# Cross-attention queries computed by rows, partly in seven products, and turned by transposes; third head's keys ahead of the first values

## The chip, the cores and the metric

The kernel runs on one core of a Trainium2 chip. The metric is the device time of one execution in microseconds (us), as a median of several runs. A profile is one further execution, recorded by the hardware profiler; its span goes from the first to the last instruction. The engines are named as the profile does: PE (TensorE, matrix products; PEld its weight loads), DVE (VectorE), ACT (ScalarE), POOL (GpSimd) and SP (SyncE, which issues the DMAs).

## What is computed

One encoder block on x (256 rows of 2048) with memory mem (256 rows of 2048), all in f32:

```python
x = x + 0.5 * swiglu(rms_norm(x, ffn1_norm), w_gate, w_up, w_down)      # 2048 -> 5632 -> 2048
x = x + concat(pool_mixer, gla_mixer)(rms_norm(x, mix_norm) @ w_in) @ w_out
x = x + mem_cross_attention(rms_norm(x, xattn_norm), rms_norm(mem, mem_norm), w_q, w_kv, w_o)
x = x + 0.5 * swiglu(rms_norm(x, ffn2_norm), ...)
out = rms_norm(x, final_norm)

def mem_cross_attention(h, mem_h, w_q, w_kv, w_o):      # 4 heads of 512
    q = (h @ w_q).reshape(b, s, 4, 512)
    kv = (mem_h @ w_kv).reshape(b, 256, 2, 4, 512)
    k, v = kv[:, :, 0], kv[:, :, 1]
    p = softmax(einsum('bshd,bmhd->bhsm', q, k) * 512 ** -0.5)
    return einsum('bhsm,bmhd->bshd', p, v).reshape(b, s, 2048) @ w_o
```

The change touches the cross-attention alone.

## The kernel before

**Products in f32.** Each f32 operand is split into a rounded part and a remainder (`split`, L705: ACT casts to fp32r, DVE subtracts). A product is then three products in fp32r: high by high, high by low and low by high. The activations lie split in `xs` and `ys`, as 16 tiles of 128 features with 256 tokens, high and low side by side. Weights come from DRAM as units of 1 MB into four buffers `raw`; DVE and ACT split a unit into `wh` and `wl`.

**Three ways to go through a weight.** `block_a` (L746) works by columns: a unit is 4 tiles of features by 512 columns, the weights stand in the array, the tokens stream, and the result `pa` has features on partitions. Each of a unit's 16 weight tiles needs one product of 512 columns (high and low tokens) and one of 256 (the weights' remainder). `block_s` (L889) works by rows: a unit is 2 tiles of features by 1024 columns, 128 tokens at a time stand in the array, the weights stream, and the result `pt` has tokens on partitions. A plain unit is 24 products of 512 columns. For the pairs of tiles that its argument `pairs` names, a unit goes by sevens: a scheme like Strassen's, 7 block products instead of 8, so 21 products of 512. This needs sums of the activations (`part_sums`, L818, on DVE, in tiles `xe`, `ye` or `xx`) and sums of the weights (`split_seven`, L842: `xh` and `xl` hold the split of three quarters of the raw unit, three DVE additions make the sums in `raw`, and these are split into `wh` and `wl`). When the last such unit is done, `combine` (L967) copies and adds the extra accumulators into a tile of its own, and each half of the result is later joined with the plain accumulators on DVE (`joined_to`, L1186). The accumulators come from four PSUM tiles of two banks; a block by rows with sevens holds all four until `combine` has read two of them.

**Cross-attention before.** Four heads of queries by columns (L1726 to L1730): `ev_Q` (L1660) adds the two halves of each accumulator into a tile `c` (ACT copy, DVE add) and splits that into `ys`. Then mem, normalized by rows, is transposed into `xs` a quarter at a time (`mem_fold`, L1619, tiles `tm`), each quarter as soon as the last query block has read the tiles that it overwrites. Keys by columns into `K` (`ev_K`), logits, softmax and its transposes per head (`logits`, `probs`), values by rows with pairs 2, 4 and 6 by sevens (`V_PAIRS`, L1201), and `values` (`pv`) per head. The sequence is keys 0, keys 1, values of heads 0 and 1, keys 2, keys 3, values of heads 2 and 3.

**What sets the order.** The program is a stream of units with operations hung between them: `st.op(f, n)` runs f after n further units. From it `Plan` (L205) makes a list of tasks and orders every engine's instructions by a model of their costs and due times; TensorE takes, of the tasks that the model holds ready, the first in program order. So the whole program is ordered anew when a part of it changes. Tiles of a stage live in a scope of memory that is opened and closed with it; the cross-attention's is `s_x` (L1646: one `xh` and `xl`, three tiles `c`). Nearly all instructions carry line L552, the recorder's, so rows are told apart by their tiles.

Of the kernel before, what the change touches and what calls it, by code (L numbers as in the profile page):

```python
# [10 lines left out]
F32 = mybir.dt.float32  # L11
# [6 lines left out]
P = 128  # L18
# [548 lines left out]
def build(ctx, tc, I, out):  # L567
# [24 lines left out]
    def local(shape, dt, tag, name, bufs=1):  # L592
        return tile_of(None, shape, dt, tag, name, bufs)
# [33 lines left out]
    def ctl(name, shape):  # L627
        return whole_lines(const, shape, F32, name, name)
# [4 lines left out]
    ident = plan.fixed(eye, [P, P])  # L633
    gains = ctl("gains", [P, G_END])
    Rcol = ctl("Rcol", [P, 2])
    ss = ctl("ss", [P, 2, 8])
    sums = ctl("sums", [P, 2])
    chain = ctl("chain", [P, 3, 8])

# [247 lines left out]
                )  # L887

    def block_s(srcs, act, ext, pairs, evict, spare=None, joins=(0, 1), delays=(0, 0), order=None,  # L889
                ends=None):  # L890

# [73 lines left out]
            ends.row_factor(1)  # L965

        def combine():  # L967
            e = held["e"] = local([P, 4, NB], F32, tag="sg", name=uid("sg"), bufs=2)
            a, b = held["parts"]
            nc.scalar.copy(e[:, 0], a[:, 0])  # L970
            nc.vector.tensor_tensor(out=e[:, 3], in0=a[:, 1], in1=e[:, 0], op=ALU.add)
            nc.vector.tensor_tensor(
                out=e[:, 1:3], in0=b, in1=e[:, 3:4].to_broadcast([P, 2, NB]), op=ALU.add
            )
            nc.vector.tensor_tensor(out=e[:, 3], in0=b[:, 1], in1=e[:, 1], op=ALU.add)
            held["rest"] = {j: (e[:, 2:4], ALU.subtract) if j else (e[:, 0:2], ALU.add) for j in joins}
# [221 lines left out]
    END_ORDER = (0, 2, 1, 4, 3, 5)  # L1198
    OUT_PAIRS = (3, 4, 6)
    W_OUT_PAIRS = (3, 5, 6)  # L1200
    V_PAIRS = (2, 4, 6)  # L1201

    def sums_of(act, ext, pairs, tag, forms=3):
        t = local([P, len(pairs), 2, forms, P], F32R, tag=tag, name=uid(tag))
# [7 lines left out]
    def gate_sums():  # L1212

        sums_of(xs, xe, PAIRS, "xe")

    def ffn(wg, wu, wd, down, first=()):
        gate = {}

        def hidden():
            e = local([P, 4, NB], F32, tag="sg", name=uid("sg"), bufs=2)  # L1220
            return {0: e[:, 2:4], 1: e[:, 0:2]}

        def ev_gate(j, c, fresh):
# [12 lines left out]

        def turn(g, k):

            v = four(ptile(uid("ph")))
            for i in range(4):  # L1240
                for h in range(2):
                    nc.tensor.transpose(
                        v[:, i, h * P : (h + 1) * P], g[:, h, i * P : (i + 1) * P], ident
                    )
            split(ys[:, k : k + 4, 0, :], ys[:, k : k + 4, 1, :], v)

        for lo, n in FF_PARTS:
            for b in range(0, n - 1, 2):
                n0 = (lo + b) * NB
                pairs = first if lo == b == 0 else PAIRS  # L1250
                if pairs:
                    block_s(wwide(wg, n0), xs, xe, pairs, joined_to(lambda j, c: ev_gate(j, c, 0)))
                else:
                    block_t(wwide(wg, n0), xs, lambda j, ps: ev_gate(j, ps, 1))
                block_s(wwide(wu, n0), xs, xe, PAIRS, joined_to(ev_up))
                held = {}
                st.op(lambda held=held: held.update(gate))
                wait = PAIRS[-1] + 1 if b + 2 < n else 1
                for j in range(2):
                    st.op(lambda j=j, b=b, held=held: turn(held[j], 4 * (b + j)), wait)  # L1260
                if not b and (lo + n < FF // NB or down is down_first):
                    st.op(lambda: sums_of(ys, ye, DOWN_PAIRS, "ye"), wait)
            if n % 2:
                def both(j, c):
                    if j:
                        ev_up(0, c)
                    else:
                        ev_gate(0, c, 0)
                block_s(wtwo(wg, wu, (lo + n - 1) * NB), xs, xe, PAIRS, joined_to(both), joins=(0, 1))
                st.op(lambda n=n: turn(gate[0], 4 * (n - 1)), 1)  # L1270
            down(wd, 4 * lo, 4 * n, lo + n == FF // NB)
# [323 lines left out]
    st.op(open_scope("s_out"), 1)  # L1595


    xa = {}

    def xt(name, shape, dt=F32, tag=None, bufs=1):  # L1600
        t = whole_lines(None, shape, dt, tag or name, uid(name), bufs)
# [8 lines left out]
    def mem_norm():  # L1610
        for c in range(8):
            row_squares([xa[f"mem{h}"][:, c * S : (c + 1) * S] for h in range(2)], c)
        nc.vector.tensor_reduce(out=sums, in_=ss, axis=AX.X, op=ALU.add)
        Rm = xt("Rm", [P, 2])
        rsqrt(Rm, sums, D, 2)
        for h in range(2):
            nc.vector.tensor_scalar_mul(xa[f"mem{h}"], xa[f"mem{h}"], Rm[:, h : h + 1])
# [12 lines left out]

    xx = {}

    def mem_sums(g):
        if not xx:
            xx["all"] = local([P, len(V_PAIRS), 2, 4, P], F32R, tag="xx", name=uid("xx"))
        i = V_PAIRS.index(g)
        xx[g] = xx["all"][:, i]
        part_sums(xs, xx["all"][:, i : i + 1], (g,))

    def x_factors():  # L1640
        nc.vector.tensor_scalar_mul(xt("nR", [P, 2]), Rcol, -(XHD ** -0.5))
        nc.vector.tensor_scalar_mul(xt("sR", [P, 2]), Rcol, XHD ** -0.5)

    into_x(I["w_out"][0], ys, 1.0, G_X, spread_too=False, pairs=W_OUT_PAIRS, made=1)
    st.op(close_scope, 2)
    st.op(open_scope("s_x", 1, 3), 2)  # L1646
    st.op(x_factors, 2)
    st.op(mem_in, 2)
    st.op(mem_norm, 6)
# [4 lines left out]
    def whole(ps):  # L1654
# [1 line left out]
        nc.scalar.copy(c, ps[:, :, S:])  # L1656
        nc.vector.tensor_tensor(out=c, in0=ps[:, :, :S], in1=c, op=ALU.add)
        return c

    def ev_Q(h):  # L1660
        def evict(p, ps):
            split_pair(ys, 4 * h + 2 * p, whole(ps))
        return evict

    def ev_K(h):
        def evict(p, ps):
# [13 lines left out]
    def logits(h):  # L1680
        ps = ptile(uid("pl"))
        for t in range(2):
            tok = slice(t * P, (t + 1) * P)
            parts = [(d, a, b) for d in range(4) for a, b in ((0, 0), (0, 1), (1, 0))]
            for i, (d, a, b) in enumerate(parts):
                nc.tensor.matmul(
                    ps[:, t, :M], ys[:, 4 * h + d, a, tok], xa["K", h][:, d, b, :],
                    start=i == 0, stop=i == 11,
                )
        nm, sm = xt("nm", [P, 2]), xt("sm", [P, 2])  # L1690
        nc.vector.tensor_reduce(out=nm, in_=ps[:, :, :M], axis=AX.X, op=ALU.max)
        nc.vector.tensor_tensor(out=nm, in0=nm, in1=xa["nR"], op=ALU.mult)
        pr = xt("P", [P, 2, M])
        for t in range(2):
            nc.scalar.activation(
                pr[:, t, :], ps[:, t, :M], AF.Exp, scale=xa["sR"][:, t : t + 1],
                bias=nm[:, t : t + 1], accum_out=sm[:, t : t + 1],
            )
        nc.vector.reciprocal(out=sm, in_=sm)
        for t in range(2):  # L1700
            nc.vector.tensor_scalar_mul(pr[:, t, :], pr[:, t, :], sm[:, t : t + 1])

    def probs(h):
        ps = ptile(uid("pt"))
        for mtile in range(2):
            for t in range(2):
                nc.tensor.transpose(
                    ps[:, mtile, t * P : (t + 1) * P], xa["P"][:, t, mtile * P : (mtile + 1) * P], ident
                )
        PT = xa["PT", h] = xt("PT", [P, 2, 2, S], F32R, bufs=2)  # L1710
        split(PT[:, :, 0, :], PT[:, :, 1, :], ps[:, :, :S])

    def values(h):
# [9 lines left out]
                    )  # L1723
            split_pair(ys, 4 * h + 2 * p, ps[:, :, :S])

    for h in range(H):  # L1726
        if h == H - 1:
            for c in range(4):
                st.op(lambda c=c: mem_fold(c), c + 2)
        block_a(wblock(w_q, h * NB), xs, ev_Q(h))  # L1730
    for b in range(2):
        h = 2 * b
        block_a(wblock(w_kv, h * NB), xs, ev_K(h))
        if not b:
            for i, g in enumerate(V_PAIRS):
                st.op(lambda g=g: mem_sums(g), 1 + i)
        st.op(lambda h=h: logits(h), 2)
        st.op(lambda h=h: probs(h), 3)
        block_a(wblock(w_kv, (h + 1) * NB), xs, ev_K(h + 1))
        st.op(lambda h=h: logits(h + 1), 1)  # L1740
        st.op(lambda h=h: probs(h + 1), 2)
        block_s(wwide(w_kv, D + h * NB), xs, xx, V_PAIRS, joined_to(ev_V(b)))
        for j in (0, 1):
            st.op(lambda h=h, j=j: values(h + j), 1)
# [169 lines left out]
```

## Time and profile before

| | |
|---|---|
| median of 3 runs | 2077.27 us (2076.41 to 2078.64) |
| the profiled execution, its own time | 2078.63 us |
| its span | 2076.5 us, granted TensorE clock 0.999 |
| busy: PE, PEld, DVE, ACT | 2064.3, 1730.3, 1822.4, 1151.6 us |
| cross-attention up to the last `pv` | about 993 to 1291 us of the span |
| DMA | 436 MB, 210 GB/s |

How to read it: a row of a group gives engine, operation, output<-inputs, shape, count, busy us, mean ns of one, and the idle time before with what ended it. A matmul's mean is its time from entry to modelled end; as they are pipelined, their pace is the distance between starts. A row of waits reads waiter <- what it waited for: us, times, longest. A row of the chain or of the timeline begins with its start and its length in us.

### The profile page before, as it was taken

The numbers are of one execution on the slowest core, as the hardware profiler recorded it, in microseconds if no ns is written. First come the engines' busy times: TensorE is split into PE (matmuls) and PEld (weight loads), VectorE is DVE, ScalarE is ACT, GpSimd is POOL, SyncE is SP. The second block draws the span as 40 slices with busy tenths as digits, with TensorE's granted clock in tenths as the row PEclk, the third lists the DMA queues.
The fourth block names the chain that finished last, engine by engine and source line by source line (L and its number), as shares of the span: only waits on it lengthen the run. The fifth ranks groups of instructions, "written<-read, shape, count | busy, mean of one in ns | idle before, by whom it ended". The sixth has DMA issues, their size and how long they took to land.

```text
span 2076.5 us, 24457 instructions
## 1 busy us (share of the span) xinstructions
PE 2064.3 (99%) x9846; PEld 1730.3 (83%) x9846; DVE 1822.4 (88%) x1618; ACT 1151.6 (55%) x1058; POOL 7.2 (0%) x37
## 2 busy tenths in 40 slices
PE   9999999999999999999999999999999999999998
PEld 7888888888888888888888888888888888888887
DVE  7999899998999977689767758998998999989996
ACT  7665455654555655456655445656554556554654
POOL 0000000000000000000000000000000000000000
PEclk9999999999999999999999999999999999999999
DMA  8556765566656755556754545665467655676564
GB/s 303 185 202 219 247 213 210 174 253 223 229 183 237 248 187 183 166 174 234 274 181 165 201 145 179 223 241 205 164 222 263 223 186 192 232 245 221 188 237 142
DMA packets 139640, 436.07 MB, mean 210 GB/s; under 512 B 9924, under 2 KB 13608, under 8 KB 139144
## 3 DMA queue, kind: packets, MB, share of 16 engines
q1 hardware_dynamic: 139208, 433.99, 60.7%
q8 instruction: 77, 1.26, 0.2%
q10 hardware_dynamic: 320, 0.53, 0.1%
q14 instruction: 35, 0.29, 0.0%
HBM read 417.71 MB, written 16.78 MB: 209 GB/s over the span
## 4 chain that ended last, share of the span: by engine, by line
PE 81%; DVE 13%; DMA 2%; ACT 2%; issue 2%; SPq 0%; DVEq 0%; ACTq 0%
PE pt L552 61%; PE pa L552 15%; DVE wl L552 5%; DVE raw L552 3%; PE pb L552 2%; DVE xl L552 2%; DVE sg L552 1%; DMA raw<-in_ffn_w_down 1%; ACT wh L552 1%; PE ph L552 1%; DMA raw<-in_ffn_w_up 1%; PE px L552 1%; PE pl L552 1%; PE pv L552 1%; ACT xh L552 0%
## 5 line engine op out<-in xcount | busy, mean ns | idle before, releaser
L552 ACT CAST wh<-raw 128x2048 fp32r<-128x2048 f32 (+2 forms) x383 | 719.3, 1886 | 570.9 <-DVE raw L552 330.2
L552 DVE TENSOR_TENSOR wl<-raw,wh 128x2048 fp32r<-128x2048 f32 (+2 forms) x382 | 856.3, 2259 | 127.3 <-ACT wh L552 124.9
L552 PE MATMUL pt<-wh,xs 128*128 128x512 f32 x2028 | 656.0, 390 | 0.0
L552 PE MATMUL pt<-wh,ys 128*128 128x512 f32 x1508 | 477.4, 389 | 0.8 <-DVE ys L552 0.5
L552 PEld LDWEIGHTS pt<-wh,xs 128*128 128x128 f32 x2028 | 379.9, 188 | 78.7 <-DVE xs L552 0.7
L552 PE MATMUL pt<-wl,xs 128*128 128x512 f32 x1014 | 395.4, 390 | 0.4 <-DVE wl L552 0.2
L552 PEld LDWEIGHTS pt<-wh,ys 128*128 128x128 f32 x1508 | 282.7, 188 | 59.8 <-DVE ys L552 0.9
L552 DVE TENSOR_TENSOR raw<-raw 128x1024 f32<-128x1024 f32 x360 | 312.2, 867 | 8.6
L552 PE MATMUL pt<-wl,ys 128*128 128x512 f32 x754 | 293.0, 389 | 0.1
L552 ACT CAST xh<-raw 128x1536 fp32r<-128x1536 f32 x120 | 176.8, 1481 | 99.3 <-PE pt L552 38.9
L552 DVE TENSOR_TENSOR xl<-raw,xh 128x1536 fp32r<-128x1536 f32 x120 | 210.2, 1752 | 18.0 <-ACT xh L552 17.8
L552 PEld LDWEIGHTS pt<-wl,xs 128*128 128x128 f32 x1014 | 190.4, 188 | 42.6 <-DVE wl L552 3.2
L552 PE MATMUL pa<-xs,wh 128*128 128x512 f32 x912 | 220.4, 392 | 0.0
L552 PEld LDWEIGHTS pa<-xs,wh 128*128 128x128 f32 x912 | 167.2, 188 | 32.6 <-issue 0.3
L552 PEld LDWEIGHTS pt<-wl,ys 128*128 128x128 f32 x754 | 141.6, 188 | 29.6 <-DVE wl L552 0.8
L552 DVE TENSOR_TENSOR sg<-pt,sg 128x1024 f32<-128x1024 f32 (+1 forms) x155 | 149.6, 966 | 14.4 <-ACT sg L552 12.6
L552 PE MATMUL pt<-wh,xe 128*128 128x512 f32 x380 | 139.6, 390 | 0.0
L552 PE MATMUL pt<-xh,xs 128*128 128x512 f32 x344 | 120.1, 390 | 0.0
L552 PEld LDWEIGHTS pa<-xs,wl 128*128 128x128 f32 x896 | 115.0, 191 | 4.4
L552 PE MATMUL pa<-xs,wl 128*128 128x256 f32 x896 | 116.4, 283 | 0.0
L552 PEld LDWEIGHTS pt<-wh,xe 128*128 128x128 f32 x380 | 71.3, 188 | 15.0
L552 PEld LDWEIGHTS pt<-xh,xs 128*128 128x128 f32 x344 | 64.6, 188 | 13.4
(210 smaller groups left out, 1575.9 us busy)
## 6 DMA issues: line engine op xcount, KB each, us to landing
raw<-in_ffn_w_down SPq DMA_DIRECT2D x88, 1024.0 KB, 5.4
raw<-in_ffn_w_up SPq DMA_DIRECT2D x80, 1024.0 KB, 5.1
raw<-in_ffn_w_gate SPq DMA_DIRECT2D x77, 1024.0 KB, 5.0
raw<-in_w_in SPq DMA_DIRECT2D x32, 1024.0 KB, 5.3
raw<-in_xattn_w_kv SPq DMA_DIRECT2D x32, 1024.0 KB, 5.2
raw<-in_w_out SPq DMA_DIRECT2D x16, 1024.0 KB, 5.4
raw<-in_xattn_w_q SPq DMA_DIRECT2D x16, 1024.0 KB, 6.8
raw<-in_xattn_w_o SPq DMA_DIRECT2D x16, 1024.0 KB, 5.4
```

The costliest lines, as they stand in the source:

```text
L552: return f(*(real(a) for a in args), **{k: real(a) for k, a in kw.items()})
```

## The change

Queries go by rows: two blocks of 1024 columns, the first with pairs 4 and 6 by sevens, the second with 2, 4 and 6. Their sums are made by `own_sums`, as those of the values are. `combine` writes into a tile of tag `PT` instead of `sg`. The joined result has tokens on partitions, so each head is brought into `ys` by eight transposes and a split (`turn`, which moves out of `ffn`; tiles `ph`), a unit after its block. The folds of mem are hung after the seventh and eighth unit of the second block and after the first of the keys. The third head's keys come ahead of the first values, and its logits after eight units more, behind the values. The first values get a fourth pair (0) by sevens, the second keep three. Five small tiles move into the unused half of the line of `ss`, scope `s_x` has two tiles `c`, `PT` holds two heads in one tile with a single buffer, and `xx` four pairs.

```diff
-    ss = ctl("ss", [P, 2, 8])
+    ss = ctl("ss", [P, 4, 8])
+    ss, small = ss[:, :2], ss[:, 2:]
...
     def block_s(srcs, act, ext, pairs, evict, spare=None, joins=(0, 1), delays=(0, 0), order=None,
-                ends=None):
+                ends=None, hold=("sg", 2)):
...
-            e = held["e"] = local([P, 4, NB], F32, tag="sg", name=uid("sg"), bufs=2)
+            e = held["e"] = local([P, 4, NB], F32, tag=hold[0], name=uid(hold[0]), bufs=hold[1])
...
-    V_PAIRS = (2, 4, 6)
+    V_PAIRS = (0, 2, 4, 6)
+    Q_PAIRS = (2, 4, 6)
+    Q_AT = (2, 3, 4)
+    FOLD_AT = (7, 7, 8, 9)
+    TURN_AT = ((1, 1), (1, 1))
...
+    def turn(g, k):
+        v = four(ptile(uid("ph")))
+        for i in range(4):
+            for h in range(2):
+                nc.tensor.transpose(
+                    v[:, i, h * P : (h + 1) * P], g[:, h, i * P : (i + 1) * P], ident
+                )
+        split(ys[:, k : k + 4, 0, :], ys[:, k : k + 4, 1, :], v)
...
-    xa = {}
+    xa = {
+        n: small[:, i // 4, 2 * (i % 4) : 2 * (i % 4) + 2] for i, n in enumerate(("nR", "sR", "Rm", "nm", "sm"))
+    }
...
-    st.op(open_scope("s_x", 1, 3), 2)
+    st.op(open_scope("s_x", 1, 2), 2)
...
-        PT = xa["PT", h] = xt("PT", [P, 2, 2, S], F32R, bufs=2)
+        if h % 2 == 0:
+            xa["PT"] = local([P, 2, 2, 2, S], F32R, tag="PT", name=uid("PT"))
+        PT = xa["PT", h] = xa["PT"][:, h % 2]
...
-    for h in range(H):
-        if h == H - 1:
+    for i in range(len(Q_PAIRS)):
+        st.op(lambda i=i: own_sums(Q_PAIRS, i), Q_AT[i])
+    for b in range(2):
+        if b:
             for c in range(4):
-                st.op(lambda c=c: mem_fold(c), c + 2)
-        block_a(wblock(w_q, h * NB), xs, ev_Q(h))
+                st.op(lambda c=c: mem_fold(c), FOLD_AT[c])
+        block_s(wwide(w_q, 2 * b * NB), xs, xx, Q_PAIRS if b else Q_PAIRS[1:],
+                joined_to(lambda j, e, b=b: queries.update({(b, j): e})), hold=("PT", 1))
+        for j in range(2):
+            st.op(lambda b=b, j=j: turn(queries[b, j], 4 * (2 * b + j)), TURN_AT[b][j])
+    def keys(h, at):
         block_a(wblock(w_kv, h * NB), xs, ev_K(h))
...
+        st.op(lambda: logits(h), at)
+        st.op(lambda: probs(h), at + 1)
+    def all_values(b, pairs):
+        block_s(wwide(w_kv, D + 2 * b * NB), xs, xx, pairs, joined_to(ev_V(b)))
+        for h in (2 * b, 2 * b + 1):
+            st.op(lambda h=h: values(h), 1)
+    keys(0, 2)
+    keys(1, 2)
+    keys(2, 9)
+    all_values(0, V_PAIRS)
+    keys(3, 1)
+    all_values(1, V_PAIRS[1:])
```

More of the change, by code (lines that the diff above doesn't have):

```diff
@@ L1235, in ev_up @@
             nc.vector.tensor_tensor(out=gate[j], in0=c, in1=gate[j], op=ALU.mult)
[L1237 to L1245, printed above, removed]
         for lo, n in FF_PARTS:
@@ L1613, in mem_norm @@
         nc.vector.tensor_reduce(out=sums, in_=ss, axis=AX.X, op=ALU.add)
-        Rm = xt("Rm", [P, 2])
+        Rm = xa["Rm"]
         rsqrt(Rm, sums, D, 2)
@@ L1631, in build, with own_sums @@
     xx = {}
-    def mem_sums(g):
-        if not xx:
+    def own_sums(pairs, i):
+        if not i:
             xx["all"] = local([P, len(V_PAIRS), 2, 4, P], F32R, tag="xx", name=uid("xx"))
-        i = V_PAIRS.index(g)
-        xx[g] = xx["all"][:, i]
-        part_sums(xs, xx["all"][:, i : i + 1], (g,))
+        xx[pairs[i]] = xx["all"][:, i]
+        part_sums(xs, xx["all"][:, i : i + 1], pairs[i : i + 1])
     def x_factors():
-        nc.vector.tensor_scalar_mul(xt("nR", [P, 2]), Rcol, -(XHD ** -0.5))
-        nc.vector.tensor_scalar_mul(xt("sR", [P, 2]), Rcol, XHD ** -0.5)
+        nc.vector.tensor_scalar_mul(xa["nR"], Rcol, -(XHD ** -0.5))
+        nc.vector.tensor_scalar_mul(xa["sR"], Rcol, XHD ** -0.5)
     into_x(I["w_out"][0], ys, 1.0, G_X, spread_too=False, pairs=W_OUT_PAIRS, made=1)
     st.op(close_scope, 2)
-    st.op(open_scope("s_x", 1, 3), 2)
+    st.op(open_scope("s_x", 1, 2), 2)
     st.op(x_factors, 2)
@@ L1658, in whole @@
         return c
[L1660 to L1663, printed above, removed]
     def ev_K(h):
@@ L1689, in logits @@
                 )
-        nm, sm = xt("nm", [P, 2]), xt("sm", [P, 2])
+        nm, sm = xa["nm"], xa["sm"]
         nc.vector.tensor_reduce(out=nm, in_=ps[:, :, :M], axis=AX.X, op=ALU.max)
@@ L1724, in values @@
             split_pair(ys, 4 * h + 2 * p, ps[:, :, :S])
-    for h in range(H):
-        if h == H - 1:
-            for c in range(4):
-                st.op(lambda c=c: mem_fold(c), c + 2)
-        block_a(wblock(w_q, h * NB), xs, ev_Q(h))
-    for b in range(2):
-        h = 2 * b
-        block_a(wblock(w_kv, h * NB), xs, ev_K(h))
[L1734 to L1744, printed above, removed]
+    queries = {}
+    for i in range(len(Q_PAIRS)):
+        st.op(lambda i=i: own_sums(Q_PAIRS, i), Q_AT[i])
+    for b in range(2):
+        if b:
+            for c in range(4):
+                st.op(lambda c=c: mem_fold(c), FOLD_AT[c])
[4 more added lines that the diff above has]
+    def keys(h, at):
+        block_a(wblock(w_kv, h * NB), xs, ev_K(h))
+        if not h:
+            for i in range(len(V_PAIRS)):
+                st.op(lambda i=i: own_sums(V_PAIRS, i), 1 + i)
+        st.op(lambda: logits(h), at)
[10 more added lines that the diff above has]
+    all_values(1, V_PAIRS[1:])
     st.op(close_scope, 1)
```

## Prediction

> **What bounds the kernel now.** I read the page's busy times first, then TensorE's waits, then the chain of waits between 980 and 1300 us, where the cross-attention runs.
>
> ```profile
> PE 2064.3 (99%) x9846; PEld 1730.3 (83%) x9846; DVE 1822.4 (88%) x1618; ACT 1151.6 (55%) x1058; POOL 7.2 (0%) x37
> ```
> ```profile
> PE busy L552 <- POOL ident masks.py:199: 1.4, 1, 1.4
> PE px L552 <- DMA x<-in_x: 1.1, 1, 1.1
> PE pt L552 <- DVE xe L552: 0.5, 1, 0.5
> PE pt L552 <- DVE ys L552: 0.5, 1, 0.5
> PE pt L552 <- DVE xs L552: 0.3, 1, 0.3
> PE pt L552 <- DVE wl L552: 0.2, 1, 0.2
> ```
> ```profile
> 998.62 1.75 PE px L552 x16
> 1000.36 72.37 PE pa L552 x416
> 1072.73 0.87 PE tm L552 x8
> 1086.50 2.80 PE pa L552 x16
> 1135.31 5.44 PE pt L552 x24
> ```
>
> TensorE is busy for 99% of the span, and these six rows are all that it waits for as a matmul: 4.0 us, of which 2.5 are the start of the program. In the chain one product follows the other (start us, length, count). So the time here is a count of products by the pace of each, as long as the other engines keep up.
>
> Paces, from those rows: a unit of the old query blocks (16 products of 512 columns and 16 of 256) takes 72.37 / 13 = 5.567 us. A plain unit by rows (24 products of 512) takes 5.44. A 128x128 transpose takes 1.75 / 16 = 0.109. The unit by sevens (21 products) has two prices. The rows below are starts of products, first in the first feed-forward network, then in the second block of cross-attention values:
>
> ```profile
> 269.48 0.39 PE L552 MATMUL pt<-xh,xs 128*128 128x512 f32 x1
> 284.44 0.39 PE L552 MATMUL pt<-xh,xs 128*128 128x512 f32 x1
> ```
> ```profile
> 1159.68 0.40 PE L552 MATMUL pt<-xh,xs 128*128 128x512 f32 x1
> 1161.77 0.63 PE L552 MATMUL pt<-wh,xx 128*128 128x512 f32 x2
> 1163.85 0.39 PE L552 MATMUL pt<-wh,xs 128*128 128x512 f32 x1
> 1164.76 0.39 PE L552 MATMUL pt<-wl,xs 128*128 128x512 f32 x1
> 1180.29 1.07 PE L552 MATMUL pa<-xs,wh 128*128 128x512 f32 x4
> ```
>
> In the network two units by sevens and a plain one lie between the rows: 14.96 us, so (14.96 - 5.44) / 2 = 4.76 each, 0.227 a product. In the values two of each lie between 1159.68 and 1180.29: (20.61 - 10.88) / 2 = 4.87, 0.232 a product. Inside such a unit the nine products with xh or xl take 2.09 us and the nine with xx 2.08 (0.232), while the next four, with wh, wl and xs alone, take 0.91 (0.2275). So the slower ones are those that touch the tiles of scope s_x.
>
> **The change, part by part.**
>
> *Queries.* Removed: 16 units of 5.567 = 89.07 us. Added: 16 units by rows, of which five go by sevens (two pairs in the first block, three in the second): 11 x 5.44 = 59.84, and 5 x 4.76 = 23.80 or 5 x 4.87 = 24.35; also 32 transposes x 0.109 = 3.50. That is -1.93 or -1.38 us.
>
> *Values.* The first block's fourth pair turns a plain unit into one by sevens: -0.68 or -0.57.
>
> *The other six units by sevens* of the values stay. If their price falls to the network's, that is 6 x 0.11 = -0.66; otherwise 0. The diff lays scope s_x out anew: five small tiles leave it, PT becomes one tile, c has two buffers, xx four pairs. In the built programs xh, xl and xx begin on multiples of 2048 bytes before, and after at 1664 bytes past one, as xh, xl and xe do in the first network. That the place sets the pace is a guess; I take 4.76, since it is the price of the stage that is laid out so, and keep 4.87 for the range.
>
> Sum on TensorE: -3.27 us, or -1.95 at the old price.
>
> *What hides the work of the other engines.* Each added unit by sevens gives DVE another remainder (xl) and three additions, each pair of columns its sums, each block a combination and two joins:
>
> ```profile
> L552 DVE TENSOR_TENSOR wl<-raw,wh 128x2048 fp32r<-128x2048 f32 x49 | 111.6, 2288 | 44.8 <-ACT wh L552 44.7
> L552 DVE TENSOR_TENSOR c<-pa,c 128x512 f32<-128x512 f32 x16 | 10.6, 686 | 16.9 <-ACT c L552 16.9
> L552 DVE TENSOR_TENSOR xl<-raw,xh 128x1536 fp32r<-128x1536 f32 x6 | 10.5, 1756 | 7.5 <-ACT xh L552 7.5
> L552 DVE TENSOR_TENSOR raw<-raw 128x512 f32<-128x512 f32 x12 | 8.3, 691 | 0.4
> L552 DVE TENSOR_TENSOR raw<-raw 128x1024 f32<-128x1024 f32 x6 | 7.3, 1223 | 0.1
> L552 DVE TENSOR_TENSOR sg<-pt,sg 128x1024 f32<-128x1024 f32 x6 | 7.3, 1222 | 0.3
> L552 DVE TENSOR_TENSOR ys<-c,ys 128x512 fp32r<-128x512 f32 x8 | 5.4, 683 | 0.0
> L552 DVE TENSOR_TENSOR T<-xs 128x256 f32<-128x256 f32 x6 | 2.3, 419 | 0.1
> L552 DVE TENSOR_TENSOR xx<-T,xx 128x512 fp32r<-128x512 f32 x3 | 2.1, 685 | 0.0
> L552 DVE SCALAR_TENSOR_TENSOR T<-T 128x128 f32<-128x128 f32 x6 | 1.8, 292 | 0.2
> L552 DVE TENSOR_TENSOR T<-T 128x128 f32<-128x128 f32 x6 | 1.7, 287 | 0.1
> ```
> ```profile
> 300.00:350.00 50.00, 50.00 (x223) 41.39 (x222) 48.15 (x37) 30.18 (x23) 0.00 (x0) 1.00 0.54 188
> 993.00:1087.00 94.00, 94.00 (x556) 83.51 (x555) 62.22 (x71) 56.37 (x89) 0.00 (x0) 1.00 0.66 224
> 1193.00:1219.00 26.00, 26.00 (x152) 22.98 (x151) 12.26 (x9) 11.39 (x10) 0.00 (x0) 1.00 0.43 138
> ```
> ```profile
> 980.85 6.69 DVE L552 TENSOR_TENSOR wl<-raw,wh 128x2048 fp32r<-128x2048 f32 x3
> ```
>
> The windows give, after the length, busy us of PE, PEld, DVE and ACT. The query stretch (993 to 1087) has 62.2 us of DVE in 94. To it come 5 x (1.756 + 1.223 + 2 x 0.691) = 21.8 for the sevens, 3 x 2.63 = 7.9 for the sums (2.3 + 2.1 + 1.8 + 1.7 over three pairs), the first block's combination 2 x 0.691 + 1.222 = 2.6, two joins and two remainders behind the transposes 4 x 1.22 = 4.9; seven c and six ys go, -8.9. That is 90.5 us in about 92. Three remainders follow each other in 6.69 us where three means make 6.86, so 90.5 of busy time needs some 88.3: 96%, as in the network (48.15 of 50), where TensorE waits for nothing. So I cost it at nothing, but with little to spare; a DVE behind time is repaid in the keys, where it has 12.26 us of work in 26. ACT gains five xh casts and loses the c copies; it has 38 us free.
>
> The order agrees that DVE is short there. On TensorE, the head of the query stage before (pa are accumulators by columns, px the fold of x):
>
> ```order
> L552 MATMUL pa_7251<-xs,wl_7206 128x256 x2
> L552 MATMUL pa_7256<-xs,wl_7206 128x256 x2
> L552 MATMUL px_7303<-ident,x_6955 128x128 x8
> L552 MATMUL px_7314<-ident,x_6955 128x128 x8
> L552 MATMUL pa_7251<-xs,wh_7225 128x512 x2
> L552 MATMUL pa_7256<-xs,wh_7225 128x512 x2
> ```
>
> and the last unit by sevens of the first query block now (pt are accumulators by rows, wh_7527 and wl_7547 its summed weights and their remainder, wh_7496 and wl_7533 those of the plain unit behind it):
>
> ```order
> L552 MATMUL pt_7270<-xl_7489,xx_7394 128x512
> L552 MATMUL pt_7270<-xh_7475,xx_7394 128x512
> L552 MATMUL pt_7473<-wh_7527,xx_7394 128x512
> L552 MATMUL pt_7459<-wh_7527,xx_7394 128x512
> L552 MATMUL pt_7251<-wh_7527,xs 128x512
> L552 MATMUL pt_7270<-wh_7496,xs 128x512
> L552 MATMUL pt_7270<-wl_7533,xs 128x512
> L552 MATMUL pt_7270<-wh_7496,xs 128x512 x2
> L552 MATMUL pt_7270<-wl_7533,xs 128x512
> L552 MATMUL pt_7270<-wh_7496,xs 128x512 x2
> L552 MATMUL pt_7270<-wl_7533,xs 128x512
> L552 MATMUL pt_7473<-wl_7547,xx_7394 128x512
> ```
>
> Three products with wh_7527 and eight of the next unit now stand ahead of the first with wl_7547, which fills TensorE for 11 x 0.227 = 2.5 us, one remainder's time (2.29).
>
> *The folds of mem* move to the end of the second query block. On DVE before (tm are the transposes of mem):
>
> ```order
> L552 TENSOR_TENSOR ys<-c_7860,ys 128x2x256
> L552 TENSOR_TENSOR wl_7938<-raw_7784,wh_7918 128x2048
> L552 SCALAR_TENSOR_TENSOR xs<-tm_7934,gains,xs 128x256 x4
> L552 TENSOR_TENSOR wl_7993<-raw_7822,wh_7973 128x2048
> L552 SCALAR_TENSOR_TENSOR xs<-tm_7989,gains,xs 128x256 x4
> ```
>
> and now (PT_7896 is the block's combination):
>
> ```order
> L552 TENSOR_TENSOR wl_7884<-raw_7812,wh_7862 128x2048
> L552 TENSOR_TENSOR PT_7896<-pt_7722,PT_7896 128x512
> L552 TENSOR_TENSOR PT_7896<-pt_7736,PT_7896 128x1024
> L552 TENSOR_TENSOR PT_7896<-pt_7736,PT_7896 128x512
> L552 SCALAR_TENSOR_TENSOR xs<-tm_7910,gains,xs 128x256 x4
> L552 TENSOR_TENSOR PT_7896<-pt_7616,PT_7896 128x1024
> L552 TENSOR_TENSOR wl_7951<-raw_7798,wh_7903 128x2048
> ```
>
> The first quarter's four cuts stand right behind the combination, and the first key product needs them. Before, that quarter's transposes ran at 1072.73, 13.8 us ahead of the keys (the row of 1086.50: sixteen query units, the fold of x and three quarters of mem end there); now fourteen products and the second quarter's transposes lie between, 14 x 0.227 + 0.87 = 4.0 us, for about 2 us of cuts. This holds if DVE is at most 2 us late.
>
> *Third keys ahead of the first values, PT in one buffer, c in two:* counts are unchanged. The third head's logits wait eight units of values, which cover them; the four key loads move ahead of eight value loads on SP's queue, consumed in the same sequence. The second half of mem now lies where the last rows of x lay, so on SP's queue its load waits for PE's transposes (over at 1000.4) and ACT's squares of x, with query loads behind it:
>
> ```profile
> 1000.60 0.97 SPq L552 DMA_DIRECT2D mem<-in_mem  x2
> 1006.01 41.66 SPq L552 DMA_DIRECT2D raw<-in_xattn_w_q  x9
> ```
>
> Before, the query load behind both was held for a buffer until 1006.01, longer than that wait will be. Nothing.
>
> *Stalls.* In the cross-attention TensorE's weight load waits at the sevens:
>
> ```profile
> PEld pt L552 <- DVE wl L552: 0.4, 2, 0.2
> ```
>
> Six units by sevens there, 0.4 us; twelve now, so I allow +0.4.
>
> *A page against the change.* The row of the transposes says this of one:
>
> ```profile
> L552 PE MATMUL tm<-ident,mem 128*128 128x128 f32 x32 | 4.1, 272 | 0.0
> ```
>
> A mean of 272 ns, yet eight start within 0.87 us, so they overlap, and the granted clock of the query stretch, with px's 16 and most of tm's 32 in it, is 1.00. The Trainium skill, "TensorE: Matmul & The Clock Gate", Part 4: PE-mode transpose, gives about 275 ns for a transpose in a kernel and says that transposes don't count as activity for the clock; by its price the sum would be 32 x 0.275 = 8.8 us for the turns, and the change a loss of 2 us. The mean agrees with that figure and the spacing doesn't; the clock here did not fall.
>
> **The rivals.**
>
> *The sevens keep the price of s_x*: -1.95 + 0.4 = -1.55 us, 2075.7. For it: every unit by sevens of this stage runs so now. Against: the tiles' places change.
>
> *DVE falls behind in the query blocks* (slower than before). If it idles for ACT as in the network (1.85 of 50, so 3.4 in 92) and all 90.5 us must be done, with the second block's combination (2.6) ahead of the folds, it needs 96.5 us of 92.1: up to 4.4 us late, at the remainders of the sevens and at the first key product. It decides from 3.3 us of lateness (1.95 at the old price); at worst -1.95 + 4.4 = +2.45, 2079.7. For it: 96%, and the pulled-ahead products. Against: the network at 48.15 of 50.
>
> *Transposes can't overlap*: 32 x 0.272 = 8.7 instead of 3.5, so -3.27 + 5.2 = +1.9, 2079.2. The 0.87 us for eight speaks against it.
>
> *More than the count*: the planner orders the whole program anew, and the waits of 0.5, 0.5, 0.3 and 0.2 us outside the start go: -3.27 - 1.5 = -4.8, 2072.5.
>
> **How the numbers follow.** Forecast: -3.27 + 0.4 = -2.9 us. The profiled execution took 2078.63 (span 2076.5 and 2.1 around it), 1.36 above the median; it would take 2075.7, and the median 2077.27 goes to 2074.4. Chances: forecast 0.50, old price 0.20, DVE behind 0.16, overlap 0.02, more than the count 0.12. The range goes from 2072.4 (the last rival) to 2078.0 (about half of DVE's worst). A measurement of this kernel tells 0.2%, 4.15 us, from no change. Only the last rival, or 1 us of spread on top of the forecast, is faster by that: 0.12. Slower by that needs over 6 us of lost time: 0.06. So 0.82 for within it.
>
> **What would show it.** Right: no pa in the query stage, units of 5.44 and 4.76, 32 transposes in 3.5 us, TensorE's waits still near 4 us, query stage near 87 us in place of 89 with the px and tm apart. A price of 4.87 is the first rival. Waits of pt or pa for DVE wl or xs between 1025 and 1085 are the second. Wrong altogether: waits of TensorE for a DMA, or a lower clock.

## The result, and the profile after

| | before | after |
|---|---|---|
| median of 18 runs | 2077.47 us (2075.64 to 2080.58) | 2081.76 us (2079.83 to 2084.46) |
| profiled execution, its span | 2078.63, 2076.5 us | 2081.83, 2079.5 us |
| first query product to first `pv` of the last two heads | 992.91 to 1284.47: 291.56 us | 993.63 to 1285.28: 291.65 us |

The ratio is 1.002 (95%: 1.0013 to 1.0026): slower by 4.3 us, where 2.9 us less were forecast. A second comparison (below, side_after) gave 1.0010 (1.0002 to 1.0019), 1.8 us by its medians. So the sign is sure, the size is 2 to 4 us. Of the runs below, one each of layout_alone, nudged_before and nudged_after ran in a slow state (2281.79 us or more, at a granted clock of 0.85 or less); these are in their medians, which they shift by at most 0.2 us, and not in the ratios.

The profiled pair divides its 3.0 us of span like this. The attention begins 0.7 us later than before and takes as long as before (0.1 us more), where 2.9 us less were forecast. The other 2.2 us come behind it, in the second feed-forward network, which the change does not touch. What one pair of traces says of the attention is firmer than what it says of the rest: folds_later and side_folds below are the same program, and their two traces differ by 0.2 us in the attention and by 4.9 us outside it.

The page's busy times, and TensorE's waits in the whole program (waiter <- what it waited for: us, times, longest):

```profile
PE 2064.7 (99%) x9732; PEld 1723.5 (83%) x9732; DVE 1859.0 (89%) x1668; ACT 1158.6 (56%) x1058; POOL 7.2 (0%) x37
```
```profile
PE pt L552 <- DVE wl L552: 2.3, 5, 0.8
PE busy L552 <- POOL ident masks.py:199: 1.4, 1, 1.4
PE pa L552 <- DVE xs L552: 1.0, 1, 1.0
PE tm L552 <- DVE xs L552: 0.9, 1, 0.9
PE pt L552 <- DVE x L552: 0.7, 2, 0.4
PE pt L552 <- DVE xs L552: 0.4, 1, 0.4
```

There are 114 products fewer, yet PE is as busy as before (2064.3): its busy time holds the first part of each stall too (a stall of 1.05 us below shows as 0.88 us of idle time). These waits rose from 4.0 to 6.7 us, and all but the one for POOL at the start are now for VectorE. Two of them, `tm` and `pa` for `xs`, are the folds of mem.

The query stage of the changed kernel, rows of TensorE in time (start, length):

```profile
993.63 0.39 PE L552 MATMUL pt<-wh,xs 128*128 128x512 f32 x1
...
999.08 1.91 PE L552 MATMUL px<-ident,x 128*128 128x128 f32 x16
1000.75 0.47 PE L552 MATMUL pt<-wh,xs 128*128 128x512 f32 x1
...
1017.19 0.39 PE L552 MATMUL pt<-xh,xs 128*128 128x512 f32 x1
...
1027.39 0.39 PE L552 MATMUL pt<-xh,xs 128*128 128x512 f32 x1
...
1043.04 1.91 PE L552 MATMUL ph<-ident,PT 128*128 128x128 f32 x16
1044.70 0.48 PE L552 MATMUL pt<-wh,xs 128*128 128x512 f32 x1
```

A unit by sevens and a plain one lie between 1017.19 and 1027.39: 10.20 us, so 10.20 - 5.44 = 4.76 for the sevens, as forecast. Sixteen transposes go by in 1.66 us. This stage runs nearly as the count says. The place where most of the count is lost is the junction of the second query block and the first keys, first on TensorE and then on VectorE:

```profile
1082.79 1.98 PE L552 MATMUL pa<-xs,wh 128*128 128x512 f32 x8
1084.61 1.11 PE L552 MATMUL pa<-xs,wl 128*128 128x256 f32 x8
1085.56 1.03 PE L552 MATMUL tm<-ident,mem 128*128 128x128 f32 x8
1087.48 1.06 PE L552 MATMUL tm<-ident,mem 128*128 128x128 f32 x8 [0.88 <-DVE xs L552]
1088.30 0.71 PE L552 MATMUL pa<-xs,wh 128*128 128x512 f32 x2
1088.85 1.03 PE L552 MATMUL ph<-ident,PT 128*128 128x128 f32 x8
1089.64 1.64 PE L552 MATMUL pa<-xs,wh 128*128 128x512 f32 x6
1092.25 2.09 PE L552 MATMUL pa<-xs,wh 128*128 128x512 f32 x8 [0.97 <-DVE xs L552]
```
```profile
1080.14 0.48 DVE L552 SCALAR_TENSOR_TENSOR xs<-tm,gains,xs 128x256 fp32r<-128x256 f32 x1 [0.43 <-ACT xs L552]
1081.16 1.27 DVE L552 SCALAR_TENSOR_TENSOR xs<-tm,gains,xs 128x256 fp32r<-128x256 f32 x3 [0.54 <-ACT xs L552]
1082.35 1.22 DVE L552 TENSOR_TENSOR PT<-pt,PT 128x1024 f32<-128x1024 f32 x1
1083.48 2.28 DVE L552 TENSOR_TENSOR wl<-raw,wh 128x2048 fp32r<-128x2048 f32 x1
1085.68 1.65 DVE L552 SCALAR_TENSOR_TENSOR xs<-tm,gains,xs 128x256 fp32r<-128x256 f32 x4
1087.25 1.21 DVE L552 TENSOR_TENSOR PT<-pt,PT 128x1024 f32<-128x1024 f32 x1
1088.38 0.86 DVE L552 SCALAR_TENSOR_TENSOR xs<-tm,gains,xs 128x256 fp32r<-128x256 f32 x2
1089.81 0.48 DVE L552 SCALAR_TENSOR_TENSOR xs<-tm,gains,xs 128x256 fp32r<-128x256 f32 x1 [0.57 <-ACT xs L552]
1090.84 2.05 DVE L552 SCALAR_TENSOR_TENSOR xs<-tm,gains,xs 128x256 fp32r<-128x256 f32 x5 [0.54 <-ACT xs L552]
```

A stall is the distance between two starts less the work in between. Eight transposes from 1085.56 need 0.87 us and the next group starts at 1087.48: 1.05 us lost. Six products from 1089.64 need 1.36 and the next starts at 1092.25: 1.25 lost. Together 2.3 us. The transposes read `mem` alone; by the program, what they wait for is an accumulator that VectorE's work on the second quarter still reads, up to 1087.33. VectorE goes from one piece to the next there (a join `PT<-pt`, a remainder `wl`, the cuts `xs<-tm`), and its only pauses are those in which it waits for ScalarE, with which it takes turns on one accumulator. The windows of the two stretches (length, then busy us of PE, PEld, DVE, ACT) say the same:

```profile
993.63:1082.79 89.16, 89.16 (x418) 74.14 (x417) 84.90 (x99) 58.85 (x84) 0.00 (x0) 1.00 0.65 229
1082.79:1093.00 10.21, 8.36 (x52) 7.00 (x51) 9.10 (x16) 7.26 (x14) 0.00 (x0) 1.00 0.32 105
```

In the query blocks VectorE is busy for 84.9 of 89.16 us and no product of TensorE shows a wait over 0.1 us. At the first keys 9.10 us of work and 0.57 + 0.54 of waits for ScalarE fill all of its 10.21 us.

Outside the attention, the stalls of the changed kernel in the first feed-forward network's start and in the second network, TensorE's rows:

```profile
10.69 0.93 PE L552 MATMUL pt<-wh,xs 128*128 128x512 f32 x2
12.47 0.50 PE L552 MATMUL pt<-wl,xs 128*128 128x512 f32 x1 [0.84 <-DVE wl L552]
...
1469.22 0.61 PE L552 MATMUL pt<-wh,xs 128*128 128x512 f32 x2
1470.37 0.50 PE L552 MATMUL pt<-wl,xs 128*128 128x512 f32 x1 [0.54 <-DVE wl L552]
...
1640.23 0.39 PE L552 MATMUL pt<-wh,xs 128*128 128x512 f32 x1
1641.02 0.50 PE L552 MATMUL pt<-wl,xs 128*128 128x512 f32 x1 [0.40 <-DVE wl L552]
```

They lose 1.33, 0.70 and 0.56 us. None of the three stands in the trace of before.

### The profile page after: what moved, and what is told of

Same layout as the page of the kernel before. It is cut to its first block, busy times and chain, and to the rows that moved or that the text cites. A ratio compares the mean times of both kernels' runs of the same rounds, so it can differ in the third digit from the quotient of the medians.

```text
span 2079.5 us, 24284 instructions
## 1 busy us (share of the span) xinstructions
PE 2064.7 (99%) x9732; PEld 1723.5 (83%) x9732; DVE 1859.0 (89%) x1668; ACT 1158.6 (56%) x1058; POOL 7.2 (0%) x37
## 3 DMA queue, kind: packets, MB, share of 16 engines
q8 instruction: 76, 1.25, 0.2%
## 4 chain that ended last, share of the span: by engine, by line
PE 88%; DVE 7%; issue 2%; ACT 1%; DMA 1%; SPq 0%; DVEq 0%; ACTq 0%
PE pt L552 71%; PE pa L552 11%; DVE wl L552 3%; PE pb L552 2%; DVE raw L552 2%; PE ph L552 1%; DMA raw<-in_ffn_w_gate 1%; DVE xl L552 1%; ACT wh L552 1%; DVE x L552 1%; PE pv L552 1%; PE pl L552 1%; PE px L552 1%; DVE sg L552 1%; DMA raw<-in_ffn_w_down 0%
## 5 line engine op out<-in xcount | busy, mean ns | idle before, releaser
L552 PE MATMUL pt<-wh,xs 128*128 128x512 f32 x2200 | 710.2, 391 | 0.8 <-DVE x L552 0.7
L552 PEld LDWEIGHTS pt<-wh,xs 128*128 128x128 f32 x2200 | 412.1, 188 | 86.8 <-issue 1.5
L552 PE MATMUL pt<-wl,xs 128*128 128x512 f32 x1100 | 429.4, 391 | 2.3 <-DVE wl L552 2.3
L552 DVE TENSOR_TENSOR raw<-raw 128x1024 f32<-128x1024 f32 x378 | 327.8, 867 | 9.4
L552 PEld LDWEIGHTS pt<-wl,xs 128*128 128x128 f32 x1100 | 206.5, 188 | 49.9 <-DVE wl L552 7.3
L552 DVE TENSOR_TENSOR xl<-raw,xh 128x1536 fp32r<-128x1536 f32 x126 | 220.0, 1751 | 24.4 <-ACT xh L552 24.4
L552 PE MATMUL pa<-xs,wh 128*128 128x512 f32 x656 | 159.7, 393 | 1.0 <-DVE xs L552 1.0
L552 PEld LDWEIGHTS pa<-xs,wh 128*128 128x128 f32 x656 | 120.0, 188 | 24.6 <-issue 1.7
L552 PEld LDWEIGHTS pa<-xs,wl 128*128 128x128 f32 x640 | 82.2, 191 | 3.2
L552 PE MATMUL pa<-xs,wl 128*128 128x256 f32 x640 | 83.2, 283 | 0.0
```

Of the source, the lines that this page charges most:

```text
L552: return f(*(real(a) for a in args), **{k: real(a) for k, a in kw.items()})
```

## The experiments

There were four comparisons of four kernels, each on one chip beside the kernel before, which took 2077.60 and 2077.66 us in the first two, 2078.88 and 2079.65 in the others. "Attention" is the distance between the two starts of the table above; "first keys" are the stalls there. Programs with the same attention (after, side_after; held_after, side_held; folds_later, side_folds) differ by 0.2 to 0.4 us in it from trace to trace.

| run | median, before's | ratio (95%) | attention | first keys |
|---|---|---|---|---|
| held_after | 2079.21, 2077.60 | 1.0007 (0.9998 to 1.0015) | 291.54 | 1.05 + 1.25 |
| held_before | 2079.45, 2077.60 | 1.0007 (0.9998 to 1.0016) | 291.53 | none |
| folds_later | 2076.75, 2077.60 | 0.9996 (0.9987 to 1.0004) | 290.50 | 0.82 |
| one_seven_less | 2076.88, 2077.60 | 0.9995 (0.9986 to 1.0004) | 290.97 | 0.83 |
| layout_alone | 2077.76, 2077.66 | 1.0000 (0.9991 to 1.0009) | 291.39 | none |
| nudged_before | 2078.20, 2077.66 | 1.0002 (0.9993 to 1.0011) | 291.79 | none |
| nudged_after | 2080.21, 2077.66 | 1.0009 (1.0000 to 1.0019) | 291.78 | 1.03 + 1.76 |
| folds_later_free | 2079.75, 2077.66 | 1.0007 (0.9998 to 1.0016) | 290.46 | 0.82 |
| last_folds_later | 2079.56, 2078.88 | 0.9999 (0.9990 to 1.0008) | 290.74 | 1.04 |
| turns_later | 2078.89, 2078.88 | 1.0001 (0.9992 to 1.0010) | 290.90 | 1.02 |
| folds_and_turns_later | 2079.04, 2078.88 | 1.0000 (0.9991 to 1.0009) | 291.11 | 1.67 |
| best_two_orders | 2078.87, 2078.88 | 1.0003 (0.9994 to 1.0011) | 290.78 | 1.68 |
| side_after | 2081.43, 2079.65 | 1.0010 (1.0002 to 1.0019) | 292.05 | 1.04 + 1.27 |
| side_held | 2080.53, 2079.65 | 1.0007 (0.9998 to 1.0016) | 291.96 | 1.05 + 1.27 |
| side_folds | 2078.54, 2079.65 | 0.9997 (0.9988 to 1.0006) | 290.68 | 0.82 |
| casts_first | 2078.63, 2079.65 | 0.9995 (0.9986 to 1.0003) | 290.13 | 0.66 |

### The order outside the attention

The changed kernel with the order of before, and the other way round. A table of ranks is put in, and the planner's choice is narrowed to it; inside the attention it chooses freely.

```diff
+ORDER = (
...
+)
...
-            q, now = waiting[e], free[e]
+            q, now = [t for t in waiting[e] if t.pin is None or t.pin[0][t.pin[1]] is t], free[e]
...
```

> The changed kernel; outside the cross-attention every engine keeps the order that the kernel before has there. Theory 1 (half of the loss is the planner's new order outside the attention: stalls of 0.8 us more at the start and 2.2 more in the second feed-forward network, in the profiled pair): 2078.8 us or less, and TensorE's gaps outside the attention those of the kernel before. Rival (those stalls are not the order's, they come with other places in memory or with chance): 2081.8, as the changed kernel.

> The kernel before; outside the cross-attention every engine keeps the order that the changed kernel has there. Theory 1: slower by the same 3 us, 2080.5, with waits of TensorE for weight remainders in the first 15 us and for x and weight remainders near 1470, 1635 and 1888 us. Rival: 2077.5, unchanged.

By the medians the change's order makes the kernel before 1.85 us slower, and before's order makes the changed kernel 2.55 us faster than its first median, which is of another comparison. Both miss theory 1's figures (2080.5, and 2078.8 or less), and both intervals still hold no change against the kernel before. The stall near 12.5 us shows what goes with the order; in held_before:

```profile
11.21 0.51 PE L600 MATMUL pt<-wh,xs 128*128 128x512 f32 x1 [0.44 <-ACT wh L600]
12.56 0.50 PE L600 MATMUL pt<-wl,xs 128*128 128x512 f32 x1 [0.84 <-DVE wl L600]
```

All four traces with the change's order (after, held_before, folds_later_free, side_after) lose 1.1 to 1.3 us at this product, and none with before's order does. Before's order has a stall of its own, near 2016 us, of 0.2 to 0.9 us, which the change's order doesn't have. These stalls go with the order. The sum does not show it: outside the attention the eleven traces with before's order take 1283.2 to 1288.1 us, and the four with the change's order 1285.4 to 1287.9. So theory 1 fits in direction, and its size stays open.

Inside the attention held_after is as the changed kernel: its waits at the first keys are the same to the tenth (1.0 us of `pa` and 0.9 of `tm` for `xs`).

A nudge of the planner, to see what an order is worth by chance:

```diff
-    MARGIN = 1.01
+    MARGIN = 1.012
```

> The kernel before with the planner's allowance for VectorE's durations 1.2% in place of 1.0%. Nothing that is computed changes, but the planner orders the whole program anew. Theory 1 in its general form (the planner's order is worth a microsecond or two by chance, in either direction): a time up to 2 us away from 2077.6, with other stalls of TensorE at other places. Rival (the order that came with the change is worse for a reason of the change): 2077.6 within 0.5 us.

> The changed kernel with the same nudge (1.2% in place of 1.0%). Theory 1: stalls outside the attention at other places than in the changed kernel, 2079 to 2083 us; the two stalls at the first keys stay as long as the folds hang where they do. Rival: 2081.8 within 0.5 us, the same stalls.

Before's kernel moves by 0.5 us, which its interval does not tell from nothing; the changed one by 1.5 from its first median, which is of another comparison and whose interval overlaps with this one's, with other stalls outside (0.73 us at 20 us, 0.53 at 277, none at 12.5) and the two at the first keys in place. So neither expectation is decided by the times; the traces show that other orders stall at other places, and that the first keys stall under both.

### Where the folds hang

With before's order outside, so that only the attention differs from held_after:

```diff
-    FOLD_AT = (7, 7, 8, 9)
+    FOLD_AT = (7, 8, 9, 10)
```

> As held_after, with the second, third and fourth fold of mem hung a unit later (7, 8, 9, 10 in place of 7, 7, 8, 9). Theory 2 (the 2.3 us at the first keys are lost because VectorE has 17 us of work in 15 there, whatever stands where): as held_after, within 0.5 us. Rival (they are lost because the folds hang too early and hold accumulators that the keys need): 1 to 2.3 us less than held_after.

```diff
-        block_s(wwide(w_q, 2 * b * NB), xs, xx, Q_PAIRS if b else Q_PAIRS[1:],
+        block_s(wwide(w_q, 2 * b * NB), xs, xx, Q_PAIRS[:2] if b else Q_PAIRS[1:],
```

> As held_after, with pairs 2 and 4 alone by sevens in the second query block, so that its combination comes two units earlier and VectorE has some 5 us less work in that block. Count: one seven fewer, +0.68 us. Theory 2: the two stalls at the first keys (1.05 and 1.25 us) go, so 1.6 us less than held_after. Rival (the folds' place): 0.7 us more than held_after, the stalls stay.

The rival won the first of these and theory 2 the second. Folds a unit later take 2.46 us off the time and 1.04 off the attention in the trace. A seven less takes 2.33 off the time, although its count is 0.68 us worse. Both differences stand out of the spread of the runs: all eleven of held_after took 2078.31 us or more, and of folds_later and one_seven_less only one and two of eleven did. So both the folds' place and VectorE's load count. In the trace the seven less shortens the attention by 0.57 us and leaves one stall, 0.83 us at the fourth head's transposes (`ph` for `xs`). One stall is left in folds_later, two products of 0.45 us and then a wait for the second quarter's cuts, 0.82 us:

```profile
1085.51 0.73 PE L600 MATMUL pa<-xs,wh 128*128 128x512 f32 x2
1086.78 2.09 PE L600 MATMUL pa<-xs,wh 128*128 128x512 f32 x8 [0.53 <-DVE xs L600]
```

The same hang with the order left to the planner:

> The changed kernel with the folds hung at 7, 8, 9 and 10, the order outside the attention left to the planner, which gives the changed kernel's order there. If the two losses add up (folds 2.5, order outside 2.5): 2081.8 - 2.5 = 2079.3. If only the held order made folds_later fast: 2081.8.

2079.75: the two losses add up as expected, 2.0 us under the changed kernel's first median and 3.0 above folds_later, with the kernel before within 0.2 us of the same median in all three comparisons. That is as far as medians of three comparisons go; its own interval holds 1.

Then the parts of the hang, each beside held_after's:

```diff
-    FOLD_AT = (7, 7, 8, 9)
+    FOLD_AT = (7, 7, 9, 10)
```

> As held_after (2079.2), with only the third and fourth fold of mem a unit later (7, 7, 9, 10). On VectorE the order up to the second quarter's cuts stays. Theory 3 (the last quarter's transposes stand on TensorE's queue where no accumulator is free yet, with ready key products behind them): the wait of tm (1.05 us) goes and most of the 1.25 us behind it, 2077.0. Rival (VectorE is late there by its load, wherever the folds hang): 2079.2.

```diff
-    TURN_AT = ((1, 1), (1, 1))
+    TURN_AT = ((1, 1), (2, 3))
```

> As held_after (2079.2), with only the turns of the third and fourth head later (2 and 3 units behind their block in place of 1 and 1), which takes 2.4 us of VectorE and two groups of transposes out of the crowded stretch; the folds hang as in the change. Theory 3: the wait of tm stays, 1.05 us, and some of the second stall, 2078.2 to 2079.2. Rival (VectorE's load): both stalls shrink together, 2077.

The next has `FOLD_AT = (7, 8, 9, 10)` and these later turns; best_two_orders has the same and nudged_before's order outside.

> As folds_later (2076.75, with one stall of 0.82 us left at the second quarter's cuts), and the turns later as well, by which the second join comes behind those cuts. Theory 3: no stall over 0.3 us at the first keys, 2076.0. Rival: the stall stays, 2076.75.

> The attention of folds_and_turns_later, and outside it the order that nudged_before has. If its order outside is worth what its times say (0.5 us more than the kernel before): 2076.5. If what its profile shows (2 us less of stalls outside the attention): 2074.

Theory 3 held for its first half and fell with its second. Without the early last folds the wait of `tm` is gone, but the key products that now come first wait 1.04 us for the same cuts. With later turns the wait of `tm` stays at 1.02 and the second stall goes. With both there should have been no stall, and there is one of 1.67, again for the second quarter's cuts:

```profile
PE pa L600 <- DVE xs L600: 1.5, 1, 1.5
```

So the place decides how much of VectorE's lateness TensorE meets, and no place tried meets less than 0.8. The ratios of these four are 0.9999 to 1.0003, and all four intervals hold 1. best_two_orders has no gain from nudged_before's order. That order had one stall behind the attention in its own trace (0.61 us near 2015), and here, unchanged, it has five of 0.5 to 1.0 us: the fewer stalls were that one trace's, not the order's.

### The tiles' place

```diff
-    ss = ctl("ss", [P, 2, 8])
+    ss = ctl("ss", [P, 4, 8])
+    ss, small = ss[:, :2], ss[:, 2:]
...
-    xa = {}
+    xa = {
+        n: small[:, i // 4, 2 * (i % 4) : 2 * (i % 4) + 2] for i, n in enumerate(("nR", "sR", "Rm", "nm", "sm"))
+    }
```

> The kernel before with one thing of the change: the five small tiles move into the line of ss, by which xh, xl and xx of the cross-attention begin 1664 bytes past a multiple of 2048 in place of on one. All orders stay. If the place sets the pace (the prediction's guess): the products with xh, xl and xx at 0.227 us each in the values in place of 0.232, each unit by sevens 0.1 us shorter, 0.6 us in all, 2077.0. Rival (the pace belongs to the stage, not to the place): 0.232, 2077.6.

The time did not move, and yet the guess about the pace is right. Rows of a unit by sevens of the values in this kernel, the one whose rows of before the prediction shows from 1159.68 on:

```profile
1160.05 0.39 PE L600 MATMUL pt<-xh,xs 128*128 128x512 f32 x1
...
1162.09 0.62 PE L600 MATMUL pt<-wh,xx 128*128 128x512 f32 x2
1162.54 0.48 PE L600 MATMUL pt<-wl,xx 128*128 128x512 f32 x1
1162.87 0.63 PE L600 MATMUL pt<-wh,xx 128*128 128x512 f32 x2
```

The nine products with xh or xl take 2.04 us, 0.227 each, where they took 2.09. But the first product with the remainder `wl` of the sums then takes 0.33 to its successor in place of 0.23. TensorE reaches it sooner, and VectorE has not finished it sooner. Behind that wait the next five products, up to 1164.03, take 0.232 each again. The first block of values, with the logits in it, takes 45.04 us (from 1135.57) in place of 45.14, the second up to the first `pv` 50.49 (from 1234.25) in place of 50.57: 0.18 us of the 0.66 that the prediction took for six units.

In the changed kernel the first block of values, now with four units by sevens, takes 41.22 us (1162.09 to 1203.31). Before, its 45.14 us held logits (one product at 1140.59 and the 23 below) and four transposes of probabilities:

```profile
1140.94 2.91 PE L552 MATMUL pl<-K,ys 128*128 128x256 f32 x23
1143.69 0.40 PE L552 MATMUL pt<-wl,xs 128*128 128x512 f32 x1
...
1148.94 0.60 PE L552 MATMUL pt<-ident,P 128*128 128x128 f32 x4
1149.30 0.48 PE L552 MATMUL pt<-xh,xs 128*128 128x512 f32 x1
```

Without their 2.86 and 0.36 us it took 41.92, so the block gains 0.70 us: the fourth pair's 0.68 and nothing to speak of from the price of the other three. The second block goes from 50.57 to 50.47.

### Side by side on one chip

> The changed kernel once more, beside the next three on one chip: 4 us slower than the kernel before, with stalls of 1.05 and 1.25 us at the first keys.

> held_after on the same chip. Theory 1 (the order outside costs about half): 2 to 2.5 us less than side_after. Rival (the order outside costs nothing that lasts): as side_after.

> folds_later on the same chip. Its profile showed 1.0 us less in the attention than held_after; its time was 2.5 us less. Theory: 1.0 to 1.5 us less than side_held here. Rival (the time is right and the profile not): 2.5 us less.

> As folds_later, with the same order on every engine, but VectorE's four cuts of a quarter of mem each wait for all four casts of it on ScalarE, so that the two engines no longer take turns on one accumulator (in folds_later VectorE idles 0.43, 0.54 and 0.54 us there between cuts and ScalarE 0.55 and 1.05). Theory (the turns make VectorE late): the stall of 0.82 us at the second quarter's cuts shrinks below 0.5. Rival (its amount of work makes it late): 0.8 us or more stays.

The edit of casts_first, on top of folds_later:

```diff
+        first = len(plan.tasks)
         for j in range(4):
             split_scaled(xs, 4 * c + j, v[:, j, :], gcol(G_MEM + 4 * c + j))
+        for t in plan.tasks[first + 1 :: 2]:
+            for p in plan.tasks[first::2]:
+                plan.dep(t, p, True)
```

side_after is 1.8 us slower than the kernel before, not 4; its stalls at the first keys are as expected. The order outside is worth 0.9 us here by the medians (2.55 across two comparisons), under theory 1's 2 to 2.5, and the intervals of side_after and side_held overlap by more than half, so 0.9 is not clear of nothing. The folds' place is worth 2.0 (2.46 before), between the two expectations. In the traces the folds' place is worth 1.28 and 1.04 us of attention: the times gain about 1 us more than the stretch shows, and where that lies stayed open. In casts_first the turns are gone and VectorE cuts two quarters in one go (a row of ScalarE, VectorE's rows, then TensorE's at the same place):

```profile
1079.59 1.57 ACT L604 ACTIVATE xs<-tm,gains 128x256 fp32r<-128x256 f32 x4
```
```profile
1081.19 1.66 DVE L604 SCALAR_TENSOR_TENSOR xs<-tm,gains,xs 128x256 fp32r<-128x256 f32 x4 [0.80 <-PE pt L604]
1082.77 2.35 DVE L604 TENSOR_TENSOR PT<-pt,PT 128x1024 f32<-128x1024 f32 x2
1085.03 2.28 DVE L604 TENSOR_TENSOR wl<-raw,wh 128x2048 fp32r<-128x2048 f32 x1
1087.23 3.37 DVE L604 SCALAR_TENSOR_TENSOR xs<-tm,gains,xs 128x256 fp32r<-128x256 f32 x8
```
```profile
1087.92 0.71 PE L604 MATMUL pa<-xs,wh 128*128 128x512 f32 x2
1089.03 2.08 PE L604 MATMUL pa<-xs,wh 128*128 128x512 f32 x8 [0.39 <-DVE xs L604]
```

The stall is 0.66 us, between the two expectations: without the turns 0.16 of 0.82 us goes. VectorE itself gains no more: it now waits once, 0.80 us, until the four casts are done (1079.59 + 1.57; the row names a product of TensorE that ended at the same moment), where it waited 0.43 and 0.54 in folds_later. So what no wait at all would be worth stays open. What is left of the stall stands behind two joins and a remainder, 4.6 us of work ahead of the second cuts. The attention is the shortest of all, 290.13, 1.4 us under before's. No version is faster than the kernel before by what the runs can tell: the best ratios are 0.9995 and 0.9996, with 1 inside.

## Why the prediction was wrong

- **Queries: right.** The stage takes 89.16 us up to the first key product. Less px (1.67), two groups of `tm` (0.83 and 0.79) and the first turns (1.66) that is 84.2 us for the sixteen units, against 83.64 forecast. The price of 4.76 and the pace of the transposes came out; about 0.1 us is lost at the first product behind each of the four groups of transposes (0.31 in place of 0.23 from 1000.75 on).
- **Transposes overlap: right.** All 32 take 1.66 + 0.79 + 0.79 = 3.24 us, 0.101 each, at a mean of 272 ns and a granted clock of 1.00. The Trainium skill, "TensorE: Matmul & The Clock Gate", Part 4: PE-mode transpose, gives about 275 ns for one of bf16 in a kernel. The mean of these, in f32, agrees; their pace is less than half of it.
- **Values, fourth pair: right.** The first block gains 0.70 us, against 0.68 forecast for the pair.
- **The other sevens at the network's price: right mechanism, wrong size.** layout_alone gives 0.18 us, not 0.66, and the changed kernel itself about 0.1. The nearest row, that of `PEld pt <- DVE wl`, already said that the sevens of the values wait for remainders; a faster product only waits longer.
- **Stalls of the sevens: right.** In the attention TensorE's weight load waits 0.8 us for remainders `wl`, 0.4 more than before, as allowed.
- **VectorE in the query blocks: right.** 95% busy against 96% forecast, and no wait of a product over 0.1 us at the sevens there. The 90.5 us left out the second block's combination (2.68 us from 1077.02 on), which the prediction counts in its rival alone; it is the last work ahead of the first quarter's. The rival's first place was empty. Nor does TensorE wait for a DMA: the load of mem and the moved key loads cost nothing.
- **The folds of mem: this step failed.** The prediction set 4.0 us of cover against 2 us of cuts, "This holds if DVE is at most 2 us late", and costed it at nothing. It followed the first quarter alone, and for that it held: its cuts end at 1082.43, and the first key product starts at 1082.79 without a wait. The other three quarters were not followed. For each, TensorE has a key unit, 5.57 us. VectorE has a remainder (2.28), a quarter's cuts (1.65), and a join or the remainder of a head's transposes (1.22): 5.15 us by these rows. Where it takes turns with ScalarE, as at the first quarter (0.43 + 0.54) and between 1089 and 1091 (0.57 + 0.54), some 1 us of waiting comes to it: an estimate of over 6 in 5.57, right behind a block that left it little slack. The line "a DVE behind time is repaid in the keys, where it has 12.26 us of work in 26" is what misled: that window of before, 1193 to 1219, has no folds in it. The price was 2.3 us of stalls of TensorE.
- **The rest of the program: left out of the sum.** The prediction had the new order only as a gain ("more than the count"). By the medians it is a loss of 0.9 us side by side and 1.85 when put into the kernel before; by the profiled pair 2.9 (0.7 ahead of the attention and 2.2 behind), which is less than two traces of one program differ by. The intervals don't settle which, nor rule out that it is nothing.
- **The rival "DVE falls behind"** named the first keys as one of its two places and a worst case of 4.4 us, and gave 2079.7. Its mechanism was the work of the sevens; what came was the folds' own.

With 2.3 us for the first keys and 0.5 for the sevens of the values, -2.9 becomes -0.1 for the attention, where the trace has +0.1. With 0.9 to 2.9 for the order it becomes +0.8 to +2.8 for the program. That covers the 1.8 us between the medians of side_after and its before, and leaves 1.5 of the first 4.3 without a place.

## What to carry to other kernels

Follow every instance of a step that moves, not the first alone: add up, unit by unit, what each engine has to do there, and take the window for the slack from a stretch with the same work. Where a planner orders the whole program, hold its order outside the edit when you time the edit, or its choices are counted as the edit's. Don't read a microsecond outside the edit off one pair of traces: two traces of one program differed by 5.1 us of span here. A faster product gains only what its next operand allows.

## What the runs showed of the hardware

- ScalarE and VectorE take turns on one accumulator. In the rows of the first keys VectorE waits 0.43, 0.54, 0.57 and 0.54 us for ScalarE's casts out of the same tile, and ScalarE 0.55 us twice for VectorE's cuts, where casts and cuts are interleaved; with the casts ahead, as in casts_first, each goes through its four in 1.6 us. The Trainium skill, "PSUM — Partial Sum Buffer", section "PSUM bank collisions raise a hardware error", says that the compiler orders any two instructions of different engines on one bank and the same quarter of its partitions, reads too. The waits agree with that; an accumulator here has two banks, and the rows don't show whether the order goes by the bank or by the whole accumulator.
- Products with xh, xl or xx take about 0.232 us where these tiles begin on multiples of 2048 bytes, and 0.227 with the same tiles 1664 bytes past one, order and work unchanged (layout_alone). Behind a wait, some products take 0.232 at the second place too. Why was not tried.
- The median of the kernel before itself went from 2077.5 to 2079.65 us from one comparison to another: 0.1%, as much as the effects asked for here. Only kernels of one comparison can be set side by side to a microsecond.
